# A mixer and feed-forward layer on one core: mask adds on another engine, new planner costs, residual rows in parts, last scalings shared

## The chip, the core and the metric

The kernel runs on one core of a Trainium2 chip. The core has a matrix engine (TensorE: PE, with its weight loads shown as PEld), a vector engine (VectorE: DVE), a scalar engine (ScalarE: ACT), a general engine (GpSimd: POOL) and SyncE (SP), which here only issues transfers. The engines run beside each other and wait for each other by semaphores; 16 DMA engines move data between the chip's memory and on-chip memory. The metric is the device time of one execution in microseconds (us); lower is better.

## What is computed

One encoder layer for 256 tokens of width 2048. Two mixers (an mLSTM and a gated delta rule, both run forwards and backwards) read one projection of the normalised input; their outputs are gated, summed and projected back, and a feed-forward block of width 8192 follows.

```python
h    = rms_norm(x, norm1_g)
proj = h @ w_in            # mLSTM q, k, v, o, i, f; delta qkv, z, a, b; two gates
y_m  = mlstm_mixer(...)    # 4 heads, chunks of 64, both directions
y_d  = gated_deltanet(...) # 8 heads, chunks of 64, triangular solves
mixed = sigmoid(g_m) * (y_m @ w_branch_m) + sigmoid(g_d) * (y_d @ w_branch_d)
x = x + mixed @ w_out
h = rms_norm(x, norm2_g)
x = x + square(relu(h @ w_ff1)) @ w_ff2
return rms_norm(x, norm_f_g)
```

## The kernel before

**Granules.** All weights are streamed once, in 512 pieces called granules (class `Gran`, list `GR`, run one after the other by `drive`). A granule is at most 128 x 1024 floats, 512 KB. SP loads it into `raw` (three buffers), ACT rounds it to `wh`, DVE computes the rest `wl` = raw - wh (four buffers each), and PE multiplies both with the activations, which are split the same way: 12 matmuls of 512 columns for a usual granule. The load, cast and subtraction of a granule stand three granules ahead of its matmuls in program order (`LA` = 3). Since there are four buffers of `wh` and `wl`, `wl` of granule i can be written once PE is done with granule i - 4.

**Order of the chunks.** zab (small projections), d (delta q, k, v), oif, mq, mk, mv (mLSTM), gd (delta gate, four parts of 8 granules, with the 24 granules d of the second delta group behind the first two), o in two halves (o0 has 8 granules of 256 columns, o1 eight of 512), gm (mLSTM gate) and bm (mLSTM branch, 4 granules for each of four column blocks), z, bd (delta branch), wo (w_out, 32 granules), f (w_ff1, 128) and y (w_ff2, 128). bm multiplies `ymT`, the transposed output of the mLSTM, which is split into `ymTh` (ACT) and `ymTl` (DVE) from `pty`, 16 transposes on PE of the rows `hm`.

**The planner.** Between the halves of the granules the mixers' work is put in: a mixer is a set of generators (`_Task`), each cut into pieces at `yield "V"` and the like. `pump` starts pieces by clocks that it estimates for PE (T), DVE (V), ACT (A) and POOL (G) with `cost` and `issue` of `_Clocks`, by priorities and by limits (`LIM`). Nothing of it is measured when the kernel runs: the numbers in `cost` set an order, and each engine then works its instructions off in that order, whatever they take. `need("ymT")` before the first bm granule forces out whatever pieces its tasks still owe, in order.

**Mixer pieces that the change touches.** `bcast_rows` fills a tile of 128 x 4 x 768 (`mm` in the mLSTM, `cmd` in each of the two groups of the delta rule) with rows by four POOL transfers and then adds masks to four of its six column blocks, four adds of 128 x 512 on POOL. `delta_solve` runs the triangular solves: 62 short steps `bs`, `xblk` on DVE. `cacc` are the convolution's accumulations on DVE, `ba` products that follow the transposed keys (`pk` on PE).

**Residual and tail.** `ld_x2` loads the residual rows x in four blocks of 512 KB on POOL's queue, `ev_f1` loads `gfb` (the last norm's gain, 1 MB) there. The last output block is made in `ff2_end`: two STTs (SCALAR_TENSOR_TENSOR) add the last products y of one token half, ACT squares them, nine short steps give 1/rms as `r`, and four scalings of 128 x 512 follow, one on ACT and three on DVE, each with its store on SP.

Nearly every recorded instruction has line L108 before and L120 after the change (the helper `call` in `_Ordered`), so tiles and not lines tell them apart.

Of the kernel before, what the change touches and what calls it, by code (L numbers as in the profile page):

```python
# [35 lines left out]
XNW = 6.0  # L36

# [6 lines left out]
class _Clocks:  # L44


    def __init__(self):
        self.t = dict(T=0.0, V=0.0, A=0.0, G=0.0)
        self.cur = None
        self.table = None  # L50
        self.quiet = False

    def cost(self, e, name, a, k):
        if name == "dma_start":
            return 1.1 if e == "G" else 0.1
        if e == "T":
            if name == "transpose":
                return 0.11
            n = a[2].free_size()
            c = 4 * max(n, 128) / 2400  # L60
            if "tile_position" in k:
                c *= max(a[1].free_size(), 32) / 128
            return c
        n = a[0].free_size()
        src = a[1] if len(a) > 1 and hasattr(a[1], "free_size") else None
        ps = src is not None and src.space == PSUM
        if e == "A":
            c = ((61 if ps else 112) + n) / 1200
            if any(hasattr(k.get(x), "free_size") for x in ("scale", "bias")):
                c += 0.093  # L70
            f = TABLES.get(a[2]) if name == "activation" else None
            if f and f != self.table:
                self.table = f
                c += 1.3
            return c
        if e == "V":
            if name == "reciprocal":
                return 0.1 + 8 * n / 960
            half = name in ("tensor_copy", "tensor_scalar") and not ps and a[0].space != PSUM
            return (66 + (n / 2 if half else n)) * 1.042e-3 + (0.06 if "scalar" in name else 0)  # L80
        return 0.1 + n * (2.2e-3 if name != "memset" else 0.9e-3)

    def issue(self, e, name, a, k):
        if self.quiet:
            return
        s = self.t[e]
        c = self.cur
        if c:
            s = max(s, c.ready(e))
        self.t[e] = s + self.cost(e, name, a, k)  # L90
        if c:
            c.end[e] = self.t[e]
            if name == "dma_start":
                c.ext = max(c.ext, self.t[e] + 2.3)
# [45 lines left out]
def layer_kernel(ctx, tc, x, xt, cst, prm, w_in, w_bm, w_bd, w_out, w_ff1, w_ff2, gf, out):  # L140
# [160 lines left out]
    def gemm(w, c0, cw, lh, ll, kt, name, evac, needs=None, pre=None, prep=None, load=None):  # L301
# [3 lines left out]
        def mk(g):  # L305
# [30 lines left out]
            return Gran(src, [2, cw], mms, 12 * cw / 2400 * 1.0125, pre_, post,  # L336
# [5 lines left out]
    def drive():  # L342
        for i in range(min(LA, len(GR))):
            GR[i].split(i)
        for i, gr in enumerate(GR):
# [7 lines left out]
            for j in range(gr.segs):  # L353
                clk.quiet = True
                next(parts, None)
                clk.quiet = False
                clk.t["T"] += seg
                if j == 0 and i + LA < len(GR):
                    pump()
                    gr.end = clk.t["T"] + seg * (gr.segs - 1)  # L360
                    GR[i + LA].split(i + LA)
                if j < gr.segs - 1:
                    pump()
# [92 lines left out]
    def bcast_rows(dram, cm, h0):  # L456
# [6 lines left out]
        G.dma_start(out=cm[:, :, 512:768], in_=rows(1, 0, 256))  # L463
        v = cm.rearrange("p h (b c) -> p h b c", c=128)
        for b0, kc in ((0, K_KF), (3, K_KB)):
            for b in (b0, b0 + 2):
                G.tensor_add(v[:, :, b, :], v[:, :, b, :],
                             cs[:, kc:kc + 128].unsqueeze(1).broadcast_to([P, 4, 128]))
# [143 lines left out]
    def mlstm_weights():  # L612
# [3 lines left out]
        bcast_rows(st["dnm"], mm, 0)  # L616
# [332 lines left out]
    def delta_solve(grp):  # L949
        yield from wait_for("G", "dcr")  # L950
        cm = pm.tile([P, 4, 768], F32, tag="cm", name="cmd")
        bcast_rows(st["dcr"], cm, grp * 4)
# [327 lines left out]
    def open_ff():  # L1280
# [10 lines left out]
        ld_x2(1)  # L1291

    def ld_x2(n):
        if n < NCH:
            c = slice(n * 512, n * 512 + 512)
            G.dma_start(out=F["x2"][:, :, c], in_=x[:, c].rearrange("(t p) c -> p t c", p=P))
# [4 lines left out]
    def ev_wo(n):  # L1301
        def ev(ps):
# [3 lines left out]
            ld_x2(n + 2)  # L1306
# [48 lines left out]
    def f1_chunk(n):  # L1355
# [15 lines left out]
        def mk(g):  # L1371
# [30 lines left out]
            return Gran(src, [2, 512], mms, 8 * (0.2267 + 0.12), pre, post)  # L1402
# [4 lines left out]
    def ev_f1(n, ps):  # L1407
        if n == 1:
            yield "G"
            G.dma_start(out=F["gfb"], in_=gf[0, :].partition_broadcast(P))  # L1410
# [47 lines left out]
    def ff2_gran(pas, ks, ns, last=False, tail=False):  # L1458


        def mm(gr, ks, k, t):
            ah, al = ahl[pas, k]
            tok = slice(t * P, t * P + P)
            for lhs, w, i in ((ah, gr.wh, 0), (ah, gr.wl, 1), (al, gr.wh, 2)):
                for n in ns:
                    j = (ks.index(k) * len(ns) + ns.index(n)) * 512
                    T.matmul(ff2_acc(n, t), lhs[:, tok], w[:, j:j + 512], start=(k == 0 and i == 0),
                             stop=(k == KF - 1 and i == 2))

        def mms(gr):  # L1470
# [9 lines left out]
            if last:  # L1480
                start(ff2_end(0), "end0")
                for g_, ks_ in held:
                    yield
                    for k in ks_:
                        mm(g_, ks_, k, 1)
# [20 lines left out]
        us = 6 * 0.216 * len(ks) * len(ns)  # L1506
# [34 lines left out]
    def ff2_end(t):  # L1541
# [25 lines left out]
        for m in range(NCH):  # L1567
            yield "A" if m == 0 else "V"
            c_ = slice(m * 512, m * 512 + 512)
            o = x2[:, t, c_]  # L1570
            if m == 0:
                A.activation(o, o, AF.Copy, scale=r)
                clk.cur.fork()
            elif m < n:
                V.tensor_scalar(o, o, r, None, op0=ALU.mult)
            else:
                V.scalar_tensor_tensor(o, o, r, gfb[:, c_], op0=ALU.mult, op1=ALU.mult)
            nc.sync.dma_start(out=out[t * P:(t + 1) * P, c_], in_=o)
# [46 lines left out]
    for n in range(NCH):  # L1625
        gemm(w_out, n * 512, 512, lambda: mT[0], lambda: mT[1], KT, f"wo{n}", ev_wo(n), needs=wo_needs)
# [73 lines left out]
```

## Time and profile before

| | before |
|---|---|
| median of 3 runs | 1494.43 us (1493.18 to 1497.01) |
| the profiled execution | 1494.89 us |
| its span | 1493.1 us |
| PE, DVE, ACT, POOL busy | 1473.5, 926.1, 765.7, 63.0 us |
| granted PE clock, mean | 0.997 of full speed |
| mean DMA rate | 192 GB/s |

The span runs from the first to the last instruction that the profiler records; 1.8 us of the profiled execution lie around it. PE is busy in 99% of the span, so what a change can bring or cost is read from the places where PE waits, where its clock falls, and from the end after the last matmul. Busy times are of single instructions; matmuls overlap, so their starts tell more than their durations.

### The profile page before, as it was taken

The page shows a single profiled execution, that of the slowest core. Times are in us where ns is not written, and L with a number is a line of the kernel's source. Part 1 is how long each engine was busy: PE and PEld are TensorE (multiplying, and loading weights), DVE is VectorE, ACT ScalarE, POOL GpSimd, SP SyncE. Part 2 cuts the span into 40 slices and gives each one's busy share as a digit, 9 for nine tenths or more (in the row PEclk, how much of TensorE's full clock was granted, in tenths as well). Part 3 has the DMA queues.
Part 4 walks back from the last instruction along what each step waited for, and adds up shares of the span by engine and source line. Part 5 has one row for each costly group of instructions (what it writes and reads, how often), then busy time and mean ns, then how long its engine had stood idle before and what let it go on. Part 6 is the DMA issues. An engine that isn't in the chain of part 4 may idle for free.

```text
span 1493.1 us, 20152 instructions
## 1 busy us (share of the span) xinstructions
PE 1473.5 (99%) x7580; PEld 1234.0 (83%) x7580; DVE 926.1 (62%) x1388; ACT 765.7 (51%) x1124; POOL 63.0 (4%) x101
## 2 busy tenths in 40 slices
PE   8999999999999999999999999999999999999997
PEld 7788788887878888888888888888888888888886
DVE  5658785369678846565655555555555555555865
ACT  5866545364755455443544443443444444444664
POOL 0020101012001100000000000000000000000000
PEclk9999999999999999999999999999999999999999
DMA  9766477464666854777666666666666666666664
GB/s 295 209 201 200 134 202 212 117 201 149 183 185 185 254 169 127 223 246 238 207 183 198 185 178 201 186 176 201 187 174 197 194 197 193 191 195 196 185 198 140
DMA packets 139810, 287.00 MB, mean 192 GB/s; under 512 B 9589, under 2 KB 18037, under 8 KB 139073
## 3 DMA queue, kind: packets, MB, share of 16 engines
q1 hardware_dynamic: 134816, 267.09, 60.0%
q0 software_dynamic: 4896, 18.64, 3.9%
q8 instruction: 59, 0.97, 0.3%
q14 instruction: 39, 0.31, 0.1%
HBM read 278.32 MB, written 7.36 MB: 191 GB/s over the span
## 4 chain that ended last, share of the span: by engine, by line
PE 89%; DMA 4%; DVE 3%; ACT 3%; issue 1%; ACTq 0%; DVEq 0%; SPq 0%
PE f L108 24%; PE y L108 23%; PE gm L108 6%; PE gd L108 6%; PE wo L108 5%; PE d L108 4%; PE mv L108 3%; PE bd L108 3%; PE bm L108 3%; DMA raw<-in_w_in_dram 3%; PE z L108 2%; PE o L108 2%; PE mk L108 1%; PE mq L108 1%; DVE wl L108 1%; ACT wh L108 1%
## 5 line engine op out<-in xcount | busy, mean ns | idle before, releaser
L108 DVE TENSOR_TENSOR wl<-raw,wh 128x1024 fp32r<-128x1024 f32 (+3 forms) x512 | 611.5, 1199 | 496.7 <-ACT wh L108 495.4
L108 ACT CAST wh<-raw 128x1024 fp32r<-128x1024 f32 (+3 forms) x512 | 523.6, 1026 | 580.3 <-PE f L108 162.8
L108 PE MATMUL f<-h,wh 128*128 128x512 f32 x1024 | 277.3, 394 | 0.1
L108 PEld LDWEIGHTS f<-h,wh 128*128 128x128 f32 x1024 | 176.1, 189 | 25.2 <-DVE x L108 0.7
L108 PE MATMUL y<-wh,ah 128*128 128x512 f32 x512 | 178.7, 389 | 0.0
L108 PE MATMUL y<-wl,ah 128*128 128x512 f32 x512 | 178.4, 389 | 0.0
L108 PE MATMUL y<-wh,al 128*128 128x512 f32 x512 | 178.3, 389 | 0.0
L108 PEld LDWEIGHTS f<-h,wl 128*128 128x128 f32 x1024 | 154.9, 189 | 20.3
L108 PE MATMUL f<-h,wl 128*128 128x256 f32 x1024 | 160.4, 281 | 0.0
L108 PEld LDWEIGHTS y<-wh,ah 128*128 128x128 f32 x512 | 96.1, 188 | 20.3 <-DVE u L108 0.4
L108 PEld LDWEIGHTS y<-wh,al 128*128 128x128 f32 x512 | 96.1, 188 | 20.0
L108 PEld LDWEIGHTS y<-wl,ah 128*128 128x128 f32 x512 | 96.1, 188 | 20.0
L108 PE MATMUL d<-wh,xTh 128*128 128x512 f32 x192 | 78.0, 406 | 0.0
L108 PE MATMUL d<-wl,xTh 128*128 128x512 f32 x192 | 75.3, 392 | 0.2
L108 PE MATMUL d<-wh,xTl 128*128 128x512 f32 x192 | 74.9, 390 | 0.0
L108 PE MATMUL gd<-wl,xTh 128*128 128x512 f32 x128 | 50.7, 396 | 2.2 <-DVE wl L108 2.2
L108 PE MATMUL gd<-wh,xTh 128*128 128x512 f32 x128 | 50.8, 397 | 0.0
L108 DVE TENSOR_TENSOR al<-aT,ah 128x256 fp32r<-128x256 f32 x128 | 50.8, 417 | 0.0
L108 PE MATMUL wo<-wl,mTh 128*128 128x512 f32 x128 | 50.1, 391 | 0.6 <-DVE wl L108 0.6
L108 PE MATMUL gm<-wh,xTh 128*128 128x512 f32 x128 | 50.6, 395 | 0.0
L108 PE MATMUL wo<-wh,mTh 128*128 128x512 f32 x128 | 50.5, 395 | 0.0
L108 PE MATMUL gd<-wh,xTl 128*128 128x512 f32 x128 | 50.5, 394 | 0.0
(312 smaller groups left out, 2040.2 us busy)
## 6 DMA issues: line engine op xcount, KB each, us to landing
raw<-in_w_ff_dram SPq DMA_DIRECT2D x256, 512.0 KB, 3.8
raw<-in_w_in_dram SPq DMA_DIRECT2D x160, 512.0 KB, 3.9
raw<-in_w_out_dram SPq DMA_DIRECT2D x32, 512.0 KB, 4.4
raw<-in_w_bm_dram SPq DMA_DIRECT2D x16, 512.0 KB, 4.4
raw<-in_w_bd_dram SPq DMA_DIRECT2D x16, 512.0 KB, 4.3
raw<-in_w_in_dram SPq DMA_DIRECT2D x16, 256.0 KB, 2.8
mx<-dgm POOLq DMA_DIRECT2D x4, 1024.0 KB, 7.5
raw<-in_w_in_dram SPq DMA_DIRECT2D x8, 288.0 KB, 4.0
```

The costliest lines, as they stand in the source:

```text
L108: return self._tc.keep_in_program_order(f(*a, **k))
```

## The change

The masks are added on DVE, in pieces (`yield "V"` ahead of each add, so that the planner puts them one by one). Five numbers of the planner are changed: a switch to a run of mixer matmuls costs 0.3 more, an ACT accumulation 0.19 more, a DVE step that reads the tile written just before it 0.12 more, and granules have other estimated times. The residual rows are loaded by SP, the blocks behind the first as `load` of a granule of the wo part, and gfb in four parts as `load` of f granules (SP's own order is made by the framework and stands below). The last granule of y is multiplied in two halves of 256 columns for the second token half. The four scalings start with the block that needs gfb; ACT takes two of them and DVE two; the last store of the second token half is issued by ACT.

```diff
 XNW = 6.0
+BCW = 9.0
...
         self.quiet = False
+        self.before, self.slab = {}, True
+            sw, self.slab = 0.3 if self.slab else 0.0, False
             if name == "transpose":
-                return 0.11
+                return 0.11 + sw
                 c *= max(a[1].free_size(), 32) / 128
-            return c
+            return c + sw
...
                 c += 0.093
+            if "accum_out" in k:
+                c += 0.19
...
             s = max(s, c.ready(e))
-        self.t[e] = s + self.cost(e, name, a, k)
+        w = self.cost(e, name, a, k)
+        if e == "V" and name != "dma_start":
+            if any(getattr(x, "tensor", None) is self.before.get(e) for x in a[1:]):
+                w += 0.12
+            self.before[e] = a[0].tensor
+        self.t[e] = s + w
...
             src = w[g * P:(g + 2) * P, c0:c0 + cw].rearrange("(k p) c -> p k c", p=P)
-            return Gran(src, [2, cw], mms, 12 * cw / 2400 * 1.0125, pre_, post,
+            return Gran(src, [2, cw], mms, 12 * (cw / 2400 + 0.0134), pre_, post,
...
                 clk.quiet = False
+                clk.slab = True
...
         G.dma_start(out=cm[:, :, 512:768], in_=rows(1, 0, 256))
+        clk.cur.ext = max(clk.cur.ext, clk.t["G"] + BCW)
             for b in (b0, b0 + 2):
-                G.tensor_add(v[:, :, b, :], v[:, :, b, :],
+                yield "V"
+                V.tensor_add(v[:, :, b, :], v[:, :, b, :],
...
         st["mm"] = mm
-        bcast_rows(st["dnm"], mm, 0)
+        yield from bcast_rows(st["dnm"], mm, 0)
...
         cm = pm.tile([P, 4, 768], F32, tag="cm", name="cmd")
-        bcast_rows(st["dcr"], cm, grp * 4)
+        yield from bcast_rows(st["dcr"], cm, grp * 4)
...
         ld_x2(0)
-        ld_x2(1)
     def ld_x2(n):
-        if n < NCH:
-            c = slice(n * 512, n * 512 + 512)
-            G.dma_start(out=F["x2"][:, :, c], in_=x[:, c].rearrange("(t p) c -> p t c", p=P))
+        c = slice(n * 512, n * 512 + 512)
+        nc.sync.dma_start(out=F["x2"][:, :, c], in_=x[:, c].rearrange("(t p) c -> p t c", p=P))
+    def ld_wo(n, g):
+        if n and g == 4:
+            ld_x2(n)
+            return 1.5
+        return 0.0
+    def ld_gf(n, g):
+        if n == 4 and g < 8:
+            c = slice(g * 256, g * 256 + 512)
+            nc.sync.dma_start(out=F["gfb"][:, c], in_=gf[0, c].partition_broadcast(P))
+            return 0.8
+        return 0.0
...
             yield "V"
-            ld_x2(n + 2)
...
             src = w_ff1[g * P:(g + 2) * P, n * 512:n * 512 + 512].rearrange("(k p) c -> p k c", p=P)
-            return Gran(src, [2, 512], mms, 8 * (0.2267 + 0.12), pre, post)
+            return Gran(src, [2, 512], mms, 8 * (0.2267 + 0.12), pre, post, None,
+                        lambda : ld_gf(n, g))
     def ev_f1(n, ps):
-        if n == 1:
-            yield "G"
-            G.dma_start(out=F["gfb"], in_=gf[0, :].partition_broadcast(P))
...
-        def mm(gr, ks, k, t):
+        def mm(gr, ks, k, t, lo=0, hi=512):
                     j = (ks.index(k) * len(ns) + ns.index(n)) * 512
-                    T.matmul(ff2_acc(n, t), lhs[:, tok], w[:, j:j + 512], start=(k == 0 and i == 0),
-                             stop=(k == KF - 1 and i == 2))
+                    T.matmul(ff2_acc(n, t)[:, lo:hi], lhs[:, tok], w[:, j + lo:j + hi],
+                             start=(k == 0 and i == 0), stop=(k == KF - 1 and i == 2 and hi == 512))
...
                     yield
-                    for k in ks_:
-                        mm(g_, ks_, k, 1)
+                    for c in ((0, 256), (256, 512)) if g_ is gr else ((0, 512),):
+                        for k in ks_:
+                            mm(g_, ks_, k, 1, *c)
...
             shape = [512 * len(ns)]
-        us = 6 * 0.216 * len(ks) * len(ns)
+        us = 6 * 0.2267 * len(ks) * len(ns)
...
         clk.cur.ext = clk.cur.last()
-        for m in range(NCH):
-            yield "A" if m == 0 else "V"
+        for m in (n, 0, 1, 2):
+            yield "A" if m in (0, 2) else "V"
             o = x2[:, t, c_]
-            if m == 0:
-                A.activation(o, o, AF.Copy, scale=r)
-                clk.cur.fork()
-            elif m < n:
+            if m == n:
+                V.scalar_tensor_tensor(o, o, r, gfb[:, c_], op0=ALU.mult, op1=ALU.mult)
+            elif m == 1:
             else:
-                V.scalar_tensor_tensor(o, o, r, gfb[:, c_], op0=ALU.mult, op1=ALU.mult)
-            nc.sync.dma_start(out=out[t * P:(t + 1) * P, c_], in_=o)
+                A.activation(o, o, AF.Copy, scale=r)
+            clk.cur.fork()
+            (nc.scalar if m == 2 and t == 1 else nc.sync).dma_start(out=out[t * P:(t + 1) * P, c_], in_=o)
...
     for n in range(NCH):
-        gemm(w_out, n * 512, 512, lambda: mT[0], lambda: mT[1], KT, f"wo{n}", ev_wo(n), needs=wo_needs)
+        gemm(w_out, n * 512, 512, lambda: mT[0], lambda: mT[1], KT, f"wo{n}", ev_wo(n), needs=wo_needs,
+             load=lambda g, n=n: ld_wo(n, g))
```

The planner's new costs move pieces through the whole mixer part, the first 640 us. Three places show how.

DVE, the pieces just before the first bm granule, before the change (`wl` belongs to the weight stream, `hm` and `ymTl` to the mLSTM's output, `cacc`, `ba` and `dpx` to the second delta group):

```order
L108 TENSOR_TENSOR wl<-raw,wh 128x1024
L108 SCALAR_TENSOR_TENSOR hm<-hm,rm,sgo 128x256 x4
L108 TENSOR_TENSOR wl<-raw,wh 128x1024
L108 SCALAR_TENSOR_TENSOR cacc<-cp,pr,cacc 128x256 x4
L108 TENSOR_TENSOR wl<-raw,wh 128x1024
L108 STREAM_TRANSPOSE dpx<-dpt 128x256
L108 SCALAR_TENSOR_TENSOR ymTl<-pty,pr,ymTh 128x256 x4
L108 TENSOR_TENSOR wl<-raw,wh 128x1024
L108 SCALAR_TENSOR_TENSOR ymTl<-pty,pr,ymTh 128x256 x4
```

The last four `hm` and the eight `ymTl` stand apart, with subtractions of the weight stream between them, and the solve (`bs`, `xblk`) comes after all of them. DVE, the same place after the change:

```order
L120 TENSOR_TENSOR bs<-nblk,xblk 64x112
L120 TENSOR_TENSOR xblk<-xblk,bs 64x4x28
L120 TENSOR_TENSOR bs<-nblk,xblk 64x87
L120 TENSOR_TENSOR xblk<-xblk,bs 64x3x29
L120 TENSOR_TENSOR bs<-nblk,xblk 64x60
L120 TENSOR_TENSOR xblk<-xblk,bs 64x2x30
L120 TENSOR_TENSOR bs<-nblk,xblk 64x31
L120 TENSOR_TENSOR xblk<-xblk,bs 64x31
L120 SCALAR_TENSOR_TENSOR hm<-hm,rm,sgo 128x256 x4
L120 SCALAR_TENSOR_TENSOR ymTl<-pty,pr,ymTh 128x256 x8
L120 TENSOR_TENSOR wl<-raw,wh 128x1024 x4
```

Four more steps (of widths 156 and 135) and then the `wl` of granule 154, the third bm granule, stand right above these rows. So the solve now stands ahead, and between two subtractions there are its last 12 steps, four `hm` and all eight `ymTl`.

PE, the transposes `pty` before the change (first of three places, in the third gm granule; eight more stand one granule later and four another one later):

```order
L108 MATMUL gm_1_4012<-wh,xTh 128x512
L108 MATMUL gm_1_4012<-wl,xTh 128x512
L108 MATMUL gm_1_4012<-wh,xTl 128x512
L108 MATMUL pty<-cs,hm 128x128 x4
L108 MATMUL gm_0_4011<-wh,xTh 128x512
L108 MATMUL gm_0_4011<-wl,xTh 128x512
L108 MATMUL gm_0_4011<-wh,xTl 128x512
```

PE, the same transposes after the change:

```order
L120 MATMUL gm_1_4082<-wh,xTh 128x512
L120 MATMUL gm_1_4082<-wl,xTh 128x512
L120 MATMUL gm_1_4082<-wh,xTl 128x512
L120 MATMUL pty<-cs,hm 128x128 x16
L120 MATMUL bm_0_4344<-wh,ymTh 128x512
L120 MATMUL bm_0_4344<-wl,ymTh 128x512
L120 MATMUL bm_0_4344<-wh,ymTl 128x512
```

All 16 moved to the place directly ahead of the first bm matmul, behind the last gm matmul.

DVE, the masks of the second delta group after the change (granules 117 and 118):

```order
L120 TENSOR_TENSOR wl<-raw,wh 128x1024
L120 TENSOR_TENSOR cmd<-cmd,cs 128x4x128 x3
L120 TENSOR_TENSOR wl<-raw,wh 128x1024
L120 TENSOR_TENSOR cmd<-cmd,cs 128x4x128
L120 SCALAR_TENSOR_TENSOR cacc<-cp,pr,cacc 128x256 x2
L120 TENSOR_TENSOR wl<-raw,wh 128x1024
```

Four adds joined the DVE row; POOL keeps the transfers of these tiles.

DVE, the products `ba` of the second delta group, before the change (in the o1 granules, 2.7 us of matmuls each):

```order
L108 TENSOR_TENSOR wl<-raw,wh 128x1024
L108 SCALAR_TENSOR_TENSOR cacc<-cp,pr,cacc 128x256 x4
L108 SCALAR_TENSOR_TENSOR ba<-pk,bd,cmd 128x2x256
L108 SCALAR_TENSOR_TENSOR ba<-pk,bd,cmd 128x2x128 x2
L108 SCALAR_TENSOR_TENSOR ba<-pk,bd,cmd 128x2x256 x2
L108 SCALAR_TENSOR_TENSOR ba<-pk,bd,cmd 128x2x128 x2
L108 SCALAR_TENSOR_TENSOR ba<-pk,bd,cmd 128x2x256
L108 TENSOR_TENSOR wl<-raw,wh 128x1024
```

After the change (in the o0 granules, which have half as many columns):

```order
L120 TENSOR_TENSOR wl<-raw,wh 128x512
L120 SCALAR_TENSOR_TENSOR cacc<-cp,pr,cacc 128x256 x4
L120 SCALAR_TENSOR_TENSOR ba<-pk,bd,cmd 128x2x256
L120 SCALAR_TENSOR_TENSOR ba<-pk,bd,cmd 128x2x128 x2
L120 SCALAR_TENSOR_TENSOR ba<-pk,bd,cmd 128x2x256 x2
L120 SCALAR_TENSOR_TENSOR ba<-pk,bd,cmd 128x2x128 x2
L120 SCALAR_TENSOR_TENSOR ba<-pk,bd,cmd 128x2x256 x2
L120 SCALAR_TENSOR_TENSOR ba<-pk,bd,cmd 128x2x128 x2
L120 SCALAR_TENSOR_TENSOR ba<-pk,bd,cmd 128x2x256
L120 TENSOR_TENSOR wl<-raw,wh 128x512
```

The burst came forward by some eight granules, and twelve instead of eight `ba` stand in one piece of it.

On SP, the four x blocks stand behind the seventh, seventh, ninth and eleventh load of w_out, and gfb's parts behind the twelfth, thirteenth and fourteenth (two there).

## Rows read from the trace of the kernel before

**Rows 1.** The page, section 1: busy time, share, instructions
```profile
PE 1473.5 (99%) x7580; PEld 1234.0 (83%) x7580; DVE 926.1 (62%) x1388; ACT 765.7 (51%) x1124; POOL 63.0 (4%) x101
```
**Rows 2.** Waits of PE: waited for, us in total, times, longest
```profile
PE gd L108 <- DVE wl L108: 2.2, 1, 2.2
PE ptd L108 <- ACT tmd L108: 0.9, 1, 0.9
PE nf L108 <- DVE hm L108: 0.7, 1, 0.7
PE wo L108 <- DVE wl L108: 0.6, 2, 0.4
```
**Rows 3.** Timeline of POOL, 296 to 363 us: start, us, operation, idle before
```profile
355.97 4.17 POOL L108 TENSOR_TENSOR cmd<-cmd,cs 128x512 f32<-128x512 f32 x3 [1.41 <-DMA cmd<-dcr]
360.62 1.32 POOL L108 TENSOR_TENSOR cmd<-cmd,cs 128x512 f32<-128x512 f32 x1 [0.49 <-DMA cmd<-dcr]
```
**Rows 4.** Timeline of DVE, 354 to 365 us
```profile
356.03 4.79 DVE L108 SCALAR_TENSOR_TENSOR cacc<-cp,pr,cacc 128x256 f32<-128x256 f32 x4
360.74 2.28 DVE L108 TENSOR_TENSOR wl<-raw,wh 128x1024 fp32r<-128x1024 f32 x1
```
**Rows 5.** Timeline of PE, 346 to 368 us
```profile
350.69 0.58 PE L108 MATMUL d<-wh,xTh 128*128 128x512 f32 x1
...
360.45 0.39 PE L108 MATMUL gd<-wh,xTh 128*128 128x512 f32 x1
363.08 0.50 PE L108 MATMUL gd<-wl,xTh 128*128 128x512 f32 x1 [2.23 <-DVE wl L108]
```
**Rows 6.** Windows: stretch, us, busy of PE to POOL, PEclk, DMA share, GB/s
```profile
350.00:375.00 25.00, 22.77 (x102) 17.86 (x101) 21.88 (x39) 15.03 (x22) 8.54 (x10) 0.93 0.67 205
...
1489.00:1491.00 2.00, 0.00 (x0) 0.00 (x0) 0.00 (x0) 0.00 (x0) 0.00 (x0) 0.50 1.05 402
```
**Rows 7.** Groups of DVE, forms apart: busy us, mean ns, idle before
```profile
L108 DVE TENSOR_TENSOR wl<-raw,wh 128x1024 fp32r<-128x1024 f32 x480 | 588.0, 1229 | 463.4 <-ACT wh L108 462.3
...
L108 DVE SCALAR_TENSOR_TENSOR cacc<-cp,pr,cacc 128x256 f32<-128x256 f32 x96 | 44.0, 508 | 0.4 <-ACT cacc L108 0.4
...
L108 DVE SCALAR_TENSOR_TENSOR ba<-pk,bd,cmd 128x512 f32<-128x512 f32 x16 | 11.5, 742 | 0.4 <-PE pk L108 0.4
...
L108 DVE SCALAR_TENSOR_TENSOR ba<-pk,bd,cmd 128x256 f32<-128x256 f32 x16 | 7.0, 474 | 0.0
...
L108 DVE TENSOR_TENSOR x<-x,gfb 128x512 f32<-128x512 f32 x6 | 4.1, 681 | 0.0
```
**Rows 8.** Chain that ended last, 445 to 473 us: start, us, what
```profile
455.59 2.75 PE gm L108 x12
458.34 0.44 PE pty L108 x4
...
471.95 1.13 PE bm L108 x5
```
**Rows 9.** Timeline of DVE, 448 to 512 us
```profile
448.99 1.66 DVE L108 SCALAR_TENSOR_TENSOR hm<-hm,rm,sgo 128x256 f32<-128x256 f32 x4
```
**Rows 10.** Timeline of DVE, first steps of the solve
```profile
476.94 0.23 DVE L108 TENSOR_TENSOR bs<-nblk,xblk 64x87 f32<-64x87 f32 x1
...
479.32 1.21 DVE L108 TENSOR_TENSOR wl<-raw,wh 128x1024 fp32r<-128x1024 f32 x1
```
**Rows 11.** Chain that ended last, 686 to 712 us
```profile
692.30 12.64 DMA raw<-in_w_out_dram
```
**Rows 12.** Timeline of DVE from the last matmul on
```profile
1487.23 0.88 DVE L108 TENSOR_SCALAR x<-x,r 128x512 f32<-128x512 f32 x2
1488.03 0.74 DVE L108 SCALAR_TENSOR_TENSOR x<-x,r,gfb 128x512 f32<-128x512 f32 x1
```
**Rows 13.** Timeline of ACT: a cast of the weight stream; the last scaling
```profile
459.54 1.05 ACT L108 CAST wh<-raw 128x1024 fp32r<-128x1024 f32 x1
...
1487.23 0.72 ACT L108 ACTIVATE x<-x,r 128x512 f32<-128x512 f32 x1 [0.87 <-DVE r L108]
```

## The prediction

> **What bounds the kernel now.** I read the page first: PE is busy 99% of the span [rows 1], so time can only come from the matmuls' own number (which the change leaves as it is, but for six more halves), from PE's waits, from its clock, and from the end. Then the waits of PE: apart from the start, four are worth naming, 2.2, 0.9, 0.7 and 0.6 us [rows 2]. Then the timelines around each. The whole of the kernel's slack is therefore some 6 us in 1493: the change cannot bring much more, while a reordered program can cost as much as PE is made to wait. The reader should look at how early the weight stream's `wl` is ready, since whoever works in between on DVE delays it.
>
> **The largest wait, 360 us.** POOL adds masks to `cmd` from 355.97 for 4.17 us and from 360.62 for 1.32 us [rows 3]. In just these stretches DVE is slow: four `cacc` take 4.79 us [rows 4] where a `cacc` takes 0.508 on average [rows 7], and a `wl` takes 2.28 [rows 4] instead of 1.229 [rows 7]. POOL and DVE at work together cost DVE 4.79 - 2.0 + 1.05 = 3.8 us. PE starts a matmul at 360.45 and the next at 363.08 [rows 5]; with 12 matmuls in 2.75 [rows 8], a start every 0.23 us, that is 2.4 us lost. After it the granted clock is 0.93 on average over 350 to 375 us [rows 6]; the two levels are 1.2 and 2.4 GHz, so a share of 2 x 0.07 of the 25 us, 3.5 us, ran at the lower one, which loses half of that, 1.7 us.
>
> **The change part by part.** *Masks on DVE* remove the overlap. Twelve adds of 128 x 512 come to DVE; the nearest row is the add of x and gfb with 0.681 [rows 7], so 8.2 us in all, 2.7 us per tile. In the order they stand with one or two `wl` between them, and three adds (2.0 us) in one gap between two subtractions are less than the 3.8 us that overlapping cost. A granule has 2.75 us of matmuls [rows 8] and its `wl` 1.23 [rows 7], so DVE has 1.5 us spare per granule and PE three granules of look-ahead: hidden. At 360 us the wait and the half clock go, since the burst is also placed earlier: gain 2.4 + 1.7 = 4.1; bounds 2.2 (another wait of that length loses the clock anyway and keeps 1.9) to 4.1.
>
> *New planner costs* move the pieces. The waits of `ptd` 0.9 and `nf` 0.7 [rows 2] stand where a chain of small steps or a burst of DVE ended just behind its place; in the new order these pieces have one or more granules in between: gain 1.6, bounds 0 to 1.9. Mixer matmuls come in runs; the first weight matmul after a run takes 0.58 instead of 0.39 [rows 5], about 0.15 to 0.2 of lost time each, and the order has 66 runs in place of 72: gain 0.9, bounds 0 to 1.2.
>
> *The price of the new order* is at the first bm granule. Before, the last four of the 16 `pty` start at 458.34 and take 0.44, and bm starts at 471.95 [rows 8]: over 13 us to spare. Now all 16 stand directly ahead of bm, and on DVE, behind the `wl` of granule 154, come 12 solve steps, four `hm`, eight `ymTl`. PE cannot pass: its `pty` need the last `hm`, and the first bm matmul needs `ymTh` and `ymTl`. I call S the moment at which PE has finished the last gm granule. Eight steps of widths 87 to 156 took 476.94 to 479.32 = 2.4 us [rows 10], and four narrower ones take less than half of that: 12 steps cost 3.0 to 3.4. Four `hm` cost 1.66 [rows 9]. After the last `hm` eight transposes (twice 0.44 [rows 8], 0.9) remain and bm can start. When does `wl` of 154 end? At the earliest its buffer is free one granule before S (2.75), then the cast (1.05 [rows 13]) and the subtraction (1.23) follow: S - 0.4 with their gaps. But in the solve DVE works `wl` plus four steps per granule, about as much as PE's 2.75, so it makes up nothing, and a more usual place is 1.4 after S. From the first: -0.4 + 3.1 + 1.6 + 0.9 = 5.2; from the second 7.0; less the 1.75 that 16 transposes cost PE in either order: a wait of 3.4 to 5.3 us. I take 4.6, nearer the second, as the solve stands directly ahead. A wait of 2.4 us was followed by 3.5 us at the lower clock [rows 5, 6], so this one will be too: 1.7 more. Cost 6.3, bounds 3.4 (no lower clock) to 7.5.
>
> *The `ba` burst* now stands among o0 granules of 1.36 us. Twelve `ba` are 6 x 0.742 + 6 x 0.474 = 7.3 us and four `cacc` 2.0 [rows 7], 9.3 us on DVE between two subtractions; PE has in the same time three granules of look-ahead (5.4 to 6.8 us with the gd ones) and some 4 us of `pk` and other runs. The two are about equal: cost 1.2, bounds 0 to 2.2. Before, eight `ba` with four `cacc` are 6.9 us against granules of 2.72, hidden. Elsewhere in the first half two or three places are as tight (a run of `pr`, `pq`, `ptd`, `pc` between two granules, with ACT's part of 5 us): 1.3, bounds 0 to 2.5.
>
> *Residual rows on SP.* Before, a load of w_out is on the chain for 12.64 us [rows 11], as four x blocks and gfb compete with it, and PE waits 0.6 [rows 2], 0.9 by starts. Now the loads come one at a time among the weights: gain 0.8, bounds -0.6 (an x load waits for the last `ptm` transposes, and the raw load behind it on SP waits with it) to 0.9. That wait is a new one in SP's queue, but the raw load behind it is three granules, 8 us, ahead of its use.
>
> *The tail.* Splitting the last y granule adds six matmuls of half the width; the first STT still waits for the last matmul in the order, so nothing overlaps: +0.1. Before, the first scaling is finished on DVE at about 1487.7 (two in 0.88 [rows 12]); ACT's takes 0.72 [rows 13]. Now DVE begins with the 0.74 of gfb [rows 12] and ACT with 0.72, so the first store leaves 0.25 later. From 1489 to 1491 the DMA engines are full (share 1.05, 402 GB/s [rows 6]), so what counts is the first store: +0.25, bounds -0.3 (the four scalings are over 0.3 earlier, if the last issue decides) to +0.3. Sum of the tail +0.3.
>
> The last store is moved from SP to ACT. In the rows the stores' bandwidth is used up by the end [rows 6], which leaves nothing for a second issuer. The Trainium skill, page "DMA: Bandwidth & Descriptors", section "Issuing engines are not separate DMA queues", says that starting transfers from several engines saves only the issuing engine's time, since all run on the same 16 DMA engines; the trace agrees with its 1.05. By the rule the ACT store brings 0; if SP's issuing (about half a microsecond apart, the length of a scaling) set the end, it would bring 0.4 and the tail would come to -0.1.
>
> **The sum.** Gains: 4.1 + 1.6 + 0.9 + 0.8 = 7.4. Costs: 6.3 + 1.2 + 1.3 + 0.3 = 9.1. Net +1.7 against the profiled execution of 1494.89, which is 0.46 over the median of 1494.43; counted half against each, 1494.66 + 1.7 = about 1496. A measurement of this kernel tells 0.3%, 4.5 us, from no change, and 1.7 is less. Forecast: **no measurable change**, 1496, its own range 1491 to 1498.9.
>
> **The rivals.** *Faster:* the pieces ahead of bm come early enough, because the solve and `hm` finish a granule or more before S, and the `ba` burst is covered. Then costs shrink to 0.3 + 1.3 and the net is -5.8: 1489. For it: DVE is busy 62% only [rows 1], and the look-ahead leaves it slack. Against: the order puts `hm` behind the `wl` of 154, and that cannot start before its buffer is free, one granule before S. Chance 0.15.
>
> *Slower:* the DVE queue at bm, at its long end. If DVE is late by a further granule in the solve, so that `wl` of 154 ends 3 us after S, the wait is 7 us; more wait means a longer stretch at the lower clock, by proportion with 363 us (1.7 us lost for 2.4 us of wait) up to 4 us. 7 + 4 in place of 6.3 makes the net +6.4: 1501. It decides from a `wl` of 154 more than 2.5 us after S. For it: four steps and a `wl` per granule are no less than a granule's matmuls; against: the wait before the solve is several granules with a free DVE. Chance 0.16.
>
> *The change doesn't do what it says:* the planner's numbers are better, but the planner's order at a forced flush doesn't follow them, and the tail's overlap isn't there. That is how the sum above reads already; the further case, that mask adds on DVE cost the 2.2 us of rows 2 in another place while nothing else moves, gives about 1496 to 1498 and lies in the forecast.
>
> **How the numbers follow.** Forecast 0.69, faster 0.15, slower 0.16. The forecast's unknown bounds add up to some +-4; taking half of each rival's side in, the range is 1490 to 1500.5. Chances: faster by over 0.3% (below 1489.95) 0.15, within 0.69, slower (above 1498.9) 0.16.
>
> **What would show it.** Right: POOL without additions; `cacc` at 0.5 and `wl` at 1.23 throughout; no wait of gd for `wl`; a wait of bm or `pty` for `hm` or `ymTl` of 3 to 5.5 us, and a stretch of lower clock behind it; PE busy in the stretch of o0 less than whole; no wo wait. Wrong: no wait before bm (then faster), or several waits over 2 us in the d and gd granules, which this order would then have made, or a tail whose stores all leave earlier after the last matmul than before.

## The result: slower by 0.9%

| | before | after |
|---|---|---|
| median | 1493.93 us (4 runs) | 1508.66 us (4 runs, 1507.62 to 1511.41) |
| profiled execution's span | 1493.1 us | 1505.8 us |
| ratio to before, 95% interval | 1 | 1.0093 (1.0078 to 1.0108) |

The prediction was 1496, range 1490 to 1500.5, no measurable change. The time lies outside the range, on the slow side.

The waits of PE after the change (waited for, us in total, times, longest) answer to [rows 2]:

```profile
PE pty L120 <- DVE hm L120: 7.7, 2, 7.4
...
PE pq L120 <- ACT cacc L120: 3.2, 2, 2.9
PE ptv L120 <- DVE cacc L120: 1.0, 2, 0.7
PE o L120 <- DVE wl L120: 1.0, 3, 0.3
PE oif L120 <- DVE wl L120: 0.6, 2, 0.4
```

The waits of before for `gd`, `nf` and `wo` are gone, that for `ptd` is 0.2, and one of 7.4 us stands at the place that the prediction had named. The timeline of PE there:

```profile
472.72 0.60 PE L120 MATMUL pty<-cs,hm 128*128 128x128 f32 x4
480.72 0.45 PE L120 MATMUL pty<-cs,hm 128*128 128x128 f32 x1 [7.40 <-DVE hm L120]
481.42 2.61 PE L120 MATMUL pty<-cs,hm 128*128 128x128 f32 x11 [0.26 <-DVE hm L120]
483.68 0.78 PE L120 MATMUL bm<-wh,ymTh 128*128 128x512 f32 x1
484.26 0.63 PE L120 MATMUL bm<-wl,ymTh 128*128 128x512 f32 x1
```

PE finishes gm at 472.7 (the S of the prediction) and works at the lower clock when it goes on: 11 transposes take 2.61 us, a bm matmul 0.63 instead of 0.39. The timeline of DVE says why it waits:

```profile
475.66 1.21 DVE L120 TENSOR_TENSOR wl<-raw,wh 128x1024 fp32r<-128x1024 f32 x1
476.80 0.30 DVE L120 TENSOR_TENSOR bs<-nblk,xblk 64x156 f32<-64x156 f32 x1
...
480.10 1.66 DVE L120 SCALAR_TENSOR_TENSOR hm<-hm,rm,sgo 128x256 f32<-128x256 f32 x4
481.69 0.86 DVE L120 SCALAR_TENSOR_TENSOR ymTl<-pty,pr,ymTh 128x256 fp32r<-128x256 f32 x2
```

The `wl` of granule 154 ends at 476.87, 4.15 us after S; 12 steps of the solve follow (476.80 to 480.10, 3.3 us), then `hm`. The windows (PEclk is the number behind the five busy times) of 350 to 375 us, which answers to [rows 6], and of the place at bm:

```profile
350.00:375.00 25.00, 25.00 (x121) 20.32 (x120) 17.45 (x36) 19.27 (x25) 0.15 (x2) 1.00 0.67 207
...
470.00:490.00 20.00, 12.34 (x52) 10.15 (x51) 16.82 (x39) 8.34 (x14) 4.13 (x6) 0.74 0.58 156
```

So at 350 us PE is busy for 25.00 us of 25 at full clock, where before had 22.77 at 0.93; at bm it is busy for 12.34 us of 20 at 0.74. The groups of DVE show the masks and the `cacc` of [rows 7] without POOL beside them:

```profile
L120 DVE SCALAR_TENSOR_TENSOR cacc<-cp,pr,cacc 128x256 f32<-128x256 f32 x96 | 40.6, 475 | 0.4 <-ACT cacc L120 0.4
...
L120 DVE TENSOR_TENSOR cmd<-cmd,cs 128x512 f32<-128x512 f32 x8 | 5.1, 681 | 0.0
```

**Where the 12.7 us are.** From both traces I took, for each pair of neighbouring matmuls, the time between their starts beyond the usual of their kind, and summed it by stretch (us lost to waits, switches and the lower clock):

| stretch | before | after | difference |
|---|---|---|---|
| 0 to 50 us | 3.7 | 3.8 | +0.1 |
| 50 to 150 (d, oif, mq) | 3.7 | 9.2 | +5.5 |
| 150 to 325 | 5.1 | 5.4 | +0.3 |
| 325 to 400 (masks, nf) | 7.6 | 2.6 | -5.0 |
| 400 to 450 (o) | 2.4 | 4.7 | +2.3 |
| 450 to 500 (bm) | 0.4 | 10.5 | +10.1 |
| 500 to 650 | 2.6 | 2.8 | +0.2 |
| 650 to the end (wo) | 2.9 | 1.8 | -1.1 |

Sum +12.4, and 0.1 in the tail. Two stretches carry the loss: bm, foreseen but too small, and the first 150 us, nearly not foreseen. Two runs below that keep the order of before in this first part (residual rows and tail alone; memsets) lose about 1 us less there than before did, so the 5.5 is good to about 1 us.

Of these 5.5 us, 2.9 are one wait of `pq` in d, and 1.0 are waits in oif; the rest is spread over short places. The chain (start, us, what) that leads to the wait of `pq`:

```profile
75.28 8.37 DMA raw<-in_w_in_dram
...
83.75 1.06 ACT wh L120
...
85.97 1.23 DVE kqd L120
...
87.28 1.07 ACT cacc L120
...
88.39 0.64 PE pq L120 x8
```

POOL issues four transfers of `cmd`, 1.5 MB, from 71.4 on; a load of the weight stream in the same time takes 8.37 us, its `wl` comes late, and `kqd`, which stands behind that `wl` on DVE although it doesn't need it, carries the delay to `pq` on PE. Such a load is there in every order that was run (6.3 to 9.9 us; 7.8 in before and 8.3 with the masks alone, both without a wait of `pq` at this place); what differs in the traces is what stands behind it. No run moved `kqd` alone, so this is read from the traces and not shown by an experiment.

### The profile page after: what moved, and what is told of

It is laid out like the page before. It is cut to its first block, busy times and chain, and to the rows that moved or that the text cites. A ratio compares the mean times of both kernels' runs of the same rounds, so it can differ in the third digit from the quotient of the medians.

```text
span 1505.8 us, 20144 instructions
## 1 busy us (share of the span) xinstructions
PE 1475.5 (98%) x7586; PEld 1236.0 (82%) x7586; DVE 924.5 (61%) x1398; ACT 765.7 (51%) x1124; POOL 40.3 (3%) x84
## 4 chain that ended last, share of the span: by engine, by line
PE 83%; DVE 7%; DMA 5%; ACT 4%; issue 2%; ACTq 0%; SPq 0%; DVEq 0%
PE f L120 24%; PE y L120 23%; PE wo L120 6%; PE d L120 5%; PE gd L120 5%; DMA raw<-in_w_in_dram 5%; PE gm L120 4%; PE bm L120 3%; PE bd L120 3%; PE mv L120 3%; DVE wl L120 3%; PE z L120 2%; ACT wh L120 2%; DVE ba L120 1%; PE po L120 1%
## 5 line engine op out<-in xcount | busy, mean ns | idle before, releaser
L120 PE MATMUL y<-wh,ah 128*128 128x512 f32 (+1 forms) x514 | 179.0, 388 | 0.0
L120 PE MATMUL y<-wl,ah 128*128 128x512 f32 (+1 forms) x514 | 178.8, 388 | 0.0
L120 PE MATMUL y<-wh,al 128*128 128x512 f32 (+1 forms) x514 | 178.8, 388 | 0.0
L120 PE MATMUL gm<-wl,xTh 128*128 128x512 f32 x128 | 50.0, 391 | 0.0
L120 PE MATMUL wo<-wh,mTl 128*128 128x512 f32 x128 | 49.9, 390 | 0.0
```

The lines of the kernel that those rows point to most:

```text
L120: return self._tc.keep_in_program_order(f(*a, **k))
```

## The experiments

**Is it the place of hm?** The changed kernel, with two priorities of the planner raised, so that `hm` and `ymT` come ahead of the solve. All rows before granule 144 stay.

```diff
-start(o_mul(c0, cw, sgs), "omul")
+start(o_mul(c0, cw, sgs), "omul", 0.4)
-start(mlstm_out(), "mout")
+start(mlstm_out(), "mout", 0.4)
```

> The changed kernel with one thing different: the tasks that make hm and ymT have priority 0.4 instead of 1 in the planner, so they stand ahead of the solve; pty stands 79 rows ahead of bm instead of directly ahead of it, and the masks, the ba burst and everything before granule 144 stand as in the changed kernel. Theory A (the place of hm behind the solve costs the wait of pty of 7.6 us, the 0.6 of the next one and some 1.7 us of lower clock): about 10 us less than the changed kernel, 1498 to 1499.5. Rival B (the weight stream is late by then whatever stands at bm, since wl of the gm granules is ready only 1.3 to 1.6 us ahead of its use; what is not waited for at bm is waited for in the next granules): 1504 to 1508. Rival C (the masks on DVE are the cost): no change, 1507 to 1509.

Measured: 1498.9, ratio to before 1.0031 (1.0017 to 1.0044). The changed kernel was 1.0093. Theory A holds: 10 us less. The chain there and the waits:

```profile
457.51 1.42 PE pty L120 x11
458.93 17.70 PE gm L120 x78
476.63 10.88 PE bm L120 x48
```

```profile
PE pq L120 <- ACT cacc L120: 3.7, 2, 3.4
...
PE pty L120 <- DVE hm L120: 0.3, 1, 0.3
```

bm runs on without a gap, and the wait in d is untouched. The `wl` of the gm granules are still ready only 1.5 to 4.1 us ahead of their use, and PE doesn't wait for them: rival B falls.

**Each part alone.** First residual rows and tail without the rest (edit: planner numbers and masks as before).

> The kernel before with only the residual rows on SP in parts, the split last granule and the shared last scalings; planner costs and masks as before. Theory A (these parts gain the 0.9 us of waits in wo and lose 0.1 to 0.3 in the tail): 1493.0 to 1494, faster by 0 to 1 us. Rival (x loads hold up w_out loads on SP): slower by 0.5 to 1.

Measured: 1494.18, ratio 1.0 (0.999 to 1.0009). The wait of wo is gone, but 0.9 us don't show beside what the start of the kernel varies by (this execution lost 2.3 us more than before's in its first 25 us). Neither theory falls.

Then the masks alone on DVE (`yield "V"` and `V.tensor_add`, as in the change).

> The kernel before with only the masks on DVE in pieces; planner costs, residual rows and tail as before. The order again has the 16 pty directly ahead of bm. Theory A (the order decides, not the masks' own time): the wait at bm is there, 5 to 8 us plus 1.7 to 2.6 of lower clock, the 4.1 us at 360 are gained, result 1498 to 1503. Rival C (the planner's costs are what cost): 1489 to 1492.

Measured: 1500.7, ratio 1.0045 (1.003 to 1.006). As theory A has it: the adds alone move enough that hm lands behind the solve.

```profile
PE pty L120 <- DVE hm L120: 5.1, 2, 4.9
PE pq L120 <- ACT cacc L120: 1.2, 1, 1.2
```

Then the five numbers alone.

> The kernel before with only the five planner numbers changed; masks on POOL, residual rows and tail as before. The order has the 16 pty directly ahead of bm here too. Theory A: the wait at bm is there with its lower clock (7 to 10 us), and the adds on POOL still slow DVE where they overlap; 1500 to 1506. Rival C (masks on DVE are the cost): 1490 to 1494.

Measured: 1507.8, ratio 1.0099 (1.0082 to 1.0115), slower than theory A had it and far from rival C.

```profile
PE pq L120 <- ACT cacc L120: 5.0, 3, 2.6
PE pty L120 <- DVE hm L120: 4.0, 2, 3.6
```

So either part makes the wait at bm, and the losses don't add: together they cost 0.93%, alone 0.45 and 0.99. With the numbers comes the `pq` wait in d (2.6 us here); the one of the masks alone stands at 375 us.

**What the adds on POOL cost.** The kernel before, every engine's order unchanged, memsets in place of the adds (so this kernel leaves the masks out).

```diff
-G.tensor_add(v[:, :, b, :], v[:, :, b, :], ...)
+clk.issue("G", "tensor_add", (v[:, :, b, :],), {})
+tc.keep_in_program_order(nc.gpsimd.memset(v[:, :, b, :], -30000.0))
```

> The kernel before in its own order on every engine, with one thing different: the twelve mask adds on POOL are twelve memsets of the same 128 x 512 areas to one large negative number (so the masked scores are all suppressed, and the output is not the layer's). A memset of POOL took about 0.5 us for this size where the add took 1.6. Theory A (the overlap of POOL's adds with DVE makes the wait of 2.4 us at 360 us and the 1.7 us of lower clock behind it): cacc at 0.48 and wl at 1.23 throughout, no wait of gd for wl, 1489.5 to 1491 against 1494. Rival (the burst of cacc alone makes wl late there): a wait of 1 us or more stays, 1492.5 to 1494.

Measured: 1490.61, ratio 0.9969 (0.9957 to 0.9981): 4.0 us less by the medians, 4.6 by the ratio, as theory A. DVE's row that answers to [rows 4], and POOL's to [rows 3]:

```profile
354.94 1.67 DVE L108 SCALAR_TENSOR_TENSOR cacc<-cp,pr,cacc 128x256 f32<-128x256 f32 x4
356.52 1.22 DVE L108 TENSOR_TENSOR wl<-raw,wh 128x1024 fp32r<-128x1024 f32 x1
```

```profile
354.93 0.53 POOL L468 MEMSET cmd<- 128x512 f32 x1 [1.48 <-DMA cmd<-dcr]
356.62 0.53 POOL L468 MEMSET cmd<- 128x512 f32 x1 [1.16 <-DMA cmd<-dcr]
```

Four `cacc` take 1.67 instead of 4.79, beside memsets of POOL too. The first step of the prediction was right.

**Which number, and is there a rule?** The numbers back, masks, residual rows and tail kept, `hm` first:

> The changed kernel with the planner's five numbers put back and hm, ymT ahead of the solve (priority 0.4): so the masks on DVE, the residual rows and the tail of the change, without its new costs. Theory A (the masks alone gain about 4 at 360 us and lose only by the order at bm; the first 130 us lose 4 to 6 us by the new costs): 6 to 8 us less than masks alone (1500.7), 1491.5 to 1494.5, same as before or faster by up to 3. Rival C (masks on DVE cost by themselves in the first half): 1496 to 1500.

Measured: 1493.01, ratio 0.9999 (0.999 to 1.0008). This lies in theory A's range, but no gain can be told. The trace shows 3.6 us less lost than before in 325 to 400 us, and 1.3 us more in 400 to 450, where o waits:

```profile
PE o L120 <- DVE wl L120: 1.4, 3, 0.8
PE pq L120 <- ACT cacc L120: 1.0, 1, 1.0
```

The changed kernel with the granule's time alone put back (`12 * cw / 2400 * 1.0125`, 0.953 of the new one at 512 columns, 0.90 at 256):

> The changed kernel with one of the five numbers put back, the estimated time of a granule. The order then has pty 73 to 82 rows ahead of bm and the ba burst in granules 143 and 144 instead of 128 and 129. Theory A (position of hm and of the ba burst): no wait at bm, no waits in o0; 10 to 13 us less than the changed kernel, 1494 to 1498. Rival D (the other four numbers carry the cost): 1503 to 1508.

Measured: 1492.87, ratio 0.999 (0.9981 to 0.9999). This is below theory A's range: the one number undoes the whole loss, and rival D falls. No wait at bm, none in o.

The changed kernel's masks, residual rows and tail with the 0.12 for DVE as the only number, and `hm` first:

> Masks on DVE, residual rows and tail of the change, of the planner's numbers only the 0.12 for a DVE step that reads the tile written just before it, and hm, ymT ahead of the solve. The ba burst stands at granules 150 and 151, among gm granules of 2.7 us, pty 76 to 85 rows ahead of bm. Theory A (a burst among full granules is hidden, among o0 granules it is not): nothing lost in o0, 1489 to 1492, faster than before by 2 to 5 us. Rival D (an order that differs from the tuned one loses somewhere else, whatever it gains here): 1494 to 1499.

Measured: 1499.19, ratio 1.0039 (1.0026 to 1.0051). Rival D. Up to 575 us it loses less than any other run here, then:

```profile
PE gm L120 <- ACT sgm L120: 8.1, 1, 8.1
```

```profile
591.68 5.37 PE po L120 x48
...
602.17 2.20 DVE yd L120 x8
...
604.39 0.70 ACT sgm L120
...
605.13 6.98 PE gm L120 x17
```

The eviction of a gm block needs two of four temporary tiles; the z gates still hold them until `yd` is scaled at the end of the second solve, which is now late. PE waits for the accumulator. The mixers can end too late as well as too early.

The changed kernel with the 0.12 put back to 0:

> The changed kernel with the 0.12 for DVE put back to 0. The order has pty 49 rows ahead of bm and the ba burst at granules 123 and 124, among gd granules of 2.7 us. Theory A: no wait at bm over 2 us and none in o0 from the burst, 8 to 12 us less than the changed kernel, 1496 to 1500, with the first 130 us as in the changed kernel. Rival D: 1503 to 1508.

Measured: 1509.82, ratio 1.0105 (1.009 to 1.012). My theory was wrong here, and rival D's range is just passed: pty stands 49 rows ahead of bm, and the wait moved along with it (2.4 us), while the first half lost more.

```profile
PE pq L120 <- ACT cacc L120: 4.9, 3, 3.9
PE pty L120 <- DVE hm L120: 2.4, 2, 2.0
```

The rule that I formed from this (the longer granule time lets the planner put more mixer work beside each granule, and the lead of the weight stream goes) was tried on the changed kernel with the granule's time times 0.96, 1.05 and 0.92 (one factor in the edit):

> The changed kernel with the estimated time of a granule times 0.96 (the number put back in the run before was 0.953 of the new one at 512 columns). The order has pty 56 to 98 rows ahead of bm, the ba burst at granules 146 and 147, the second solve ends at granule 172. Theory E (the corrected, longer granule time lets the planner put more mixer work beside each granule, so the mixers end earlier and the weight stream has no lead left; an estimate some per cent short leaves it the lead): 1490 to 1494. Rival D (each order is good or bad by chance): anything from 1488 to 1505.

Measured: 1497.27, ratio 1.0018 (1.0008 to 1.0027).

> The changed kernel with the estimated time of a granule times 1.05. The second solve ends at granule 149, pty stands 25 rows ahead of bm, the ba burst at granules 123 and 124. Theory E: still more work per granule, the weight stream late in many places; slower than the changed kernel, 1509 to 1520. Rival (only the place of hm at bm counts, which is better here): 1497 to 1501.

Measured: 1502.36, ratio 1.0049 (1.0033 to 1.0066).

> The changed kernel with the estimated time of a granule times 0.92. The second solve ends at granule 191, pty stands 71 to 78 rows ahead of bm. Theory E with the other bound (mixers that end late keep the temporary tiles, and a gm eviction on ACT waits for them, as in the run with the 0.12 alone, where PE waited 8.1 us): first half without waits over 1 us, then one of 5 to 15 us after 580 us; 1494 to 1505. Rival (the later the better): 1486 to 1490.

Measured: 1512.49, ratio 1.0116 (1.0101 to 1.0131).

| factor | 0.92 | 0.953 | 0.96 | 1.00 | 1.05 |
|---|---|---|---|---|---|
| us | 1512.49 | 1492.87 | 1497.27 | 1508.66 | 1502.36 |
| longest wait behind the start | gm for sgm 8.1 | pq 1.9 | pq 2.7 | pty 7.4 | pq 3.1 |

The column 0.953 is the run with the old formula. The rule falls as a law: the time does not rise with the number, 0.96 was 3 us above the range that I expected, 1.05 was 7 below and 0.92 was 7 above. What is left of it is one end, a mixer that ends late (0.92: the same wait for `sgm` as above); from 0.953 to 1.05 each order has its own waits, as rival D said.

**Do the adds on DVE cost anything?** So far they had come with another order. Here they stand on DVE ahead of the exponentials, billed to POOL's clock, and all else is in the order of before.

```diff
-G.tensor_add(v[:, :, b, :], v[:, :, b, :], ...)
+clk.issue("G", "tensor_add", (v[:, :, b, :],), {})
 yield from wait_for("A", "dgates")
+add_masks(cm)   # four V.tensor_add, billed to no clock
```

> The kernel before, with the twelve adds on DVE directly ahead of the exponentials that read their result, and the planner's clocks billed as if they stood on POOL, so that the order of everything else on every engine is that of before. Theory A (masks on DVE gain what the overlap cost, and cost nothing themselves where DVE has room; all that the change lost came from the new order): no wait of gd at 360 us, 4 us less than before minus up to 1 us in the short oif granules, 1490 to 1491.5. Rival C (the 2.7 us of adds on DVE hold up the weight stream where they stand, and ACT behind them): 1493 to 1496.

Measured: 1492.03, ratio 0.9985 (0.9977 to 0.9994): faster than before by 2.2 to 2.5 us, less than theory A had. The four `cacc` and the `wl` at 360 us, and the adds in oif:

```profile
357.42 1.66 DVE L108 SCALAR_TENSOR_TENSOR cacc<-cp,pr,cacc 128x256 f32<-128x256 f32 x4
359.00 1.22 DVE L108 TENSOR_TENSOR wl<-raw,wh 128x1024 fp32r<-128x1024 f32 x1
```

```profile
95.22 2.49 DVE L108 TENSOR_TENSOR cmd<-cmd,cs 128x512 f32<-128x512 f32 x4
```

The wait and the lower clock at 360 are gone. Some 2 us are missing against the memsets. In this trace 0.8 is a wait of mq for `wl` at 106 us, behind these adds; but it is 0.3 in the run below, with the adds at the same place, and 0.8 with the numbers alone, whose adds are on POOL. So a price of the adds is not shown, and what is missing stays open (wo waited 0.8 too, which the adds don't touch).

The same with residual rows in parts and the tail:

> The run before with the residual rows in parts and the tail of the change too, so all of the change's moves but none of its planner numbers and none of the reordering. Theory A: the 0.9 us of waits in wo go as well, the tail costs 0.1: 1489.5 to 1491, the fastest of all. Rival (residual rows and tail bring nothing, as in their own run): the same as the run before within 1 us.

Measured: 1491.97, ratio 0.9983 (0.9975 to 0.9992). The fastest of those that compute the layer, beating both kernels: 2.6 us less than before, 16 less than the change. Between it and the run before there is no difference that can be told, so the residual rows and the tail stay without a shown gain.

## Why the prediction was wrong

- **POOL's adds and the 360 us.** Predicted 4.1; the change lost 5.0 less in 325 to 400 us (with `nf`), and the memsets gained 4.0 to 4.6. Right. The adds on DVE take 0.681 as predicted.
- **ptd, nf, wo.** The waits went, as predicted: 0.9 to 0.2, 0.7 to none, 0.6 to none. For `nf` (0.6 to 0.9 in all five runs with the order of before) and wo (0.3 to 0.8 in all five with the old loads, none in the others) that is the change. For `ptd` it is luck: the five runs with the order of before have none, 0.1, 0.2, 0.9 and 1.2. wo's 0.9 isn't visible in a time of its own.
- **Fewer runs of mixer matmuls.** Predicted 0.9. The count fell as drawn up, 72 to 66, but from the first weight matmul behind a run to the next it is 0.32 us before and 0.34 after (medians), against 0.23 usually: some 0.1 a run and not 0.15 to 0.2. Six runs are worth 0.6, and no stretch of the table shows it.
- **The wait at bm: the right mechanism, mis-sized.** Predicted 4.6 of wait and 1.7 of clock, measured about 10 (7.4, 0.6, and 2.3 at the lower clock; the run with `hm` first gained 10). The term that failed is the end of `wl` of granule 154: I took 1.4 us after S as usual, it was 4.15. I had read from the solve's rows that DVE makes up nothing, and then assumed that the stream enters the solve with its lead, the time from the end of a `wl` to its use on PE. In the gm granules that lead is 1.2 to 1.6 us here, where the kernel before has 4.0 to 10.7. The run with the five numbers alone shows what that is worth. DVE has the same pieces in the same order at bm, but a lead of 4.4 to 5.3; PE finishes gm at 473.62:

```profile
472.77 1.21 DVE L120 TENSOR_TENSOR wl<-raw,wh 128x1024 fp32r<-128x1024 f32 x1
477.21 1.66 DVE L120 SCALAR_TENSOR_TENSOR hm<-hm,rm,sgo 128x256 f32<-128x256 f32 x4
477.82 0.30 PE L120 MATMUL pty<-cs,hm 128*128 128x128 f32 x1 [3.60 <-DVE hm L120]
```

  There `wl` of granule 154 ends 0.36 us after S, and `pty` waits 4.0 in all. From that end the sum's own steps give a wait of 4.2, and from 4.15 one of 8.0; measured are 4.0 and, in the changed kernel, 7.7. So the steps behind `wl` were right (12 of the solve 3.3, `hm` 1.66), and of the wait's terms the end of `wl` alone was wrong.

  Why the lead was lost is open. In the trace of the change the chain runs over the `ba` burst in o0 and then over loads:

```profile
404.36 6.38 DVE L120 SCALAR_TENSOR_TENSOR ba<-pk,bd,cmd 128x512 f32<-128x512 f32 x12
```

```profile
428.51 6.49 DMA raw<-in_w_in_dram
```

  But the burst alone doesn't explain it. With the numbers alone all sixteen `ba` stand behind the `wl` of granule 130, among the same short granules; the lead falls to 0.1 us at granules 135 and 136, as it does at 136 in before, which has no `ba` there, and is back at 5 by granule 143. What differs behind o0 is that the loads of granules 139 and 140 take 6.5 and 6.0 us after the change, 4.8 and 5.2 with the numbers alone, both beside four transfers of `nblk`; no run separates the two.

  The rival *slower* named this and its point, 2.5 us after S. It was the right case; its price of 1501 was still over 7 short, since it kept the rest of the sum. By its own proportion 7 us of wait would lose 5 at the lower clock and not 4; 2.3 was measured.
- **The first half.** Predicted 1.3 for "two or three places as tight"; 5.5 measured in 50 to 150 us. The step that failed is that I took these places for a question of an engine's own burst. A load beside POOL's `cmd` transfers takes some 8 us instead of 3.9, in before too, and `kqd`, which the new order puts on DVE behind that granule's `wl`, waits with it: 2.9 of the 5.5. The rest of the 5.5 has no single cause in the trace.
- **The o granules.** Predicted 1.2, measured 2.3, just outside the bound of 2.2. That the burst costs it is read from the place; no run moved the burst alone.
- **The tail.** Predicted +0.3; last matmul's start to the end of the span grew from 9.0 to 9.1, though the last matmul is now half as wide; from the first scaling on it grew from 5.9 to 6.1, near the 0.25 of the sum. The scalings start as drawn up, ACT and DVE side by side:

```profile
1499.73 1.33 ACT L120 ACTIVATE x<-x,r 128x512 f32<-128x512 f32 x2 [0.86 <-DVE r L120]
```

  (DVE's two take from 1499.73 to 1500.88; [rows 12, 13] had 1487.23 to 1488.77.) The four end 1.33 after `r` in place of 1.54, and the end of the span is not earlier for it. That agrees with the stores' bandwidth as the bound, which no run here separates.
- **The chances.** The rivals were right in kind. But a forecast built from gains that are single places and costs that are orders should have had its mass wider on the slow side: a gain is bounded by the wait that is there, 6 us in all; a new order's cost is not bounded by anything in the trace of before.

## What to carry to other kernels

Where a planner sets the order by estimated clocks, a better estimate is not a better order: correcting one number by 5% (10% for the short granules), beside four others, moved the time by 16 us here: with it put back the loss was gone. Separate a change's moves from its planner's numbers by keeping the old order (bill the old clock) and measure the move alone; then look at what stands behind each burst on an in-order engine, not only at how long the burst is. A stream that feeds PE should be checked for its lead at the entry of a long DVE loop, since a loop that is as long as a granule keeps the lead that it finds: 1.2 to 1.6 us from end to end of the gm granules in the changed kernel, 4.4 to 5.3 with the numbers alone.

## What was not expected of the hardware

- A DVE instruction beside an addition on POOL took 1.5 in place of 0.48 (`cacc`) and 2.28 in place of 1.22 (`wl`), beside a memset on POOL 0.48 and 1.22, no more than alone. It looks like waiting and not like a lower rate: each of the three slow `cacc` in before ended 0.3 us after the addition beside it had ended (357.56 after 357.27, 359.00 after 358.71, 360.42 after 360.14).
- The clock after a wait: after 2.2 us of wait at 360 us in before it was lower for some 3.5 us, after 2.9 us at 85 us in the changed kernel the next weight matmul took 0.50 and those behind it 0.40, full clock (granted clock 1.00 from 84 to 90 us). So a wait's length did not tell by itself whether the clock fell. Nor did it set the price: behind waits at bm of 3.6 (numbers alone), 4.9 (masks alone) and 7.4 us (the change) the lower clock cost 1.7, 1.8 and 2.3 us, by the starts of the transposes and matmuls.
- A load of 512 KB beside four transfers on POOL's queue (1.5 MB) took 7.8 us in before and 8.4 after, against a median of 3.9.
